# Moving a one-matmul fold of the sample rows' norm sums between two V column blocks of a gated layer

## Chip, cores and metric

The kernel runs on the 8 cores of one Trainium2 chip (two dies: cores 0 to 3 and 4 to 7). The metric is the device time of one execution in microseconds (us), that of the slowest core. A program on all cores has slow runs, in which one die is granted a lower TensorE clock; only fast runs are compared here.

## What is computed

Four layers of a decoder trunk. Layers 0 and 2 have a gated mixer: from `h` (1024 channels) come `u` and `v` (2048 each, after GELU), `v` is RMS-normed over its 2048 channels, mixed over the rows of a chunk of 128 rows, and gates `u`:

```python
z = jax.nn.gelu(jnp.einsum('btd,de->bte', h, w_in))
u, v = jnp.split(z, 2, axis=-1)
v = rmsnorm(v, g_v)                       # mean of squares over 2048 channels
# [...] masked mixing matrices ws, chunks of 128 rows
s = jnp.einsum('hij,bcjhe->bcihe', ws, vp) + bias
y = jnp.einsum('bte,ed->btd', u * s, w_out)
```

Each core has 2048 prompt rows, in two groups of 1024 (8 chunks of 128), and 64 "sample" rows, which form a short chunk of their own. The sample rows go with group 0, so their chunk occurs twice in the program: in layers 0 and 2 of group 0.

## The kernel before

The program is recorded as a list of operations. A list scheduler with modelled costs then gives every engine its order, and a wait is emitted for every dependency. The program treats PSUM, the memory that matmuls write, as eight banks of 512 fp32 columns. In the gated mixer four banks (4 to 7) hold the spatial sums of a chunk. V matmuls use the other four as two pairs: a "half" is 1024 columns of V (two column blocks of 512, eight matmuls each), and it takes one pair.

For a chunk of 128 rows: two halves of V, each followed by GELU and a square with its row sum on ScalarE; then the norm; then the spatial matmuls; then the gating product on VectorE. The sample rows' chunk is second in the list. It has only 64 rows, so both halves of its channels are stacked in the 128 partitions. The row sums of the two stacked halves then have to be added across partitions; a matmul with a 0/1 matrix does that. This is *the fold*: one matmul with two columns (the sum split in a high and a low bf16 part).

```python
# lines 1003 to 1023: a chunk of 128 rows
            for ci, (col0, nt, t) in enumerate(chunks):
                vb = vnb[ci % 2]
                vs = vstat[ci % 2]
                if nt == 128:
                    hv = []
                    for half in range(2):
                        bks = palloc(2, range(4), chain='v')
                        vx = vh[vx_turn % 3]
                        vx_turn += 1
                        hv.append(vx)

                        def mmv(e):
                            for q in range(2):
                                w = vu[2 * half + q]
                                for kc in range(KC):
                                    i = e.matmul(pap(bks, q * 512, (q + 1) * 512), lhsT=hB.t[:, kc, col0:col0 + nt], rhs=w.t[:, kc, :],
                                                 start=(kc == 0), stop=(kc == KC - 1))
                            return i
                        rec(PE, mmv, reads=vu[2 * half].all + vu[2 * half + 1].all + [hB.r[(kc, t)] for kc in range(KC)],
                            pt=[(bks, True)], cost=mmc(2 * KC, 512))
                        gelu_square(vx, bks, vs, half)
# [...] norm on POOL, two scalings on DVE
# lines 1031 to 1050: the sample rows' chunk
                else:
                    bks = palloc(2, range(4), chain='v')
                    vx = vh[vx_turn % 3]
# [...] mmvs: 32 matmuls, both channel halves stacked
                    rec(PE, mmvs, reads=sum((w.all for w in vu), []) + [hB.r[(kc, t)] for kc in range(KC)], pt=[(bks, True)], cost=mmc(2 * KC, 512) + 0.1)
                    gelu_square(vx, bks, vs, 0)
                    rec(DVE, lambda e: e.tensor_copy(out=hilo.t[:, 0:1], in_=vs.t[:, 0:1]), reads=vs.all, writes=hilo.all, cost=0.2)
                    rec(DVE, lambda e: e.tensor_tensor(out=hilo.t[:, 1:2], in0=vs.t[:, 0:1], in1=hilo.t[:, 0:1], op=ALU.subtract), reads=vs.all + hilo.all, writes=hilo.all, cost=0.2)
                    pf = palloc()
                    rec(PE, lambda e: e.matmul(pap(pf, 0, 2), lhsT=maskT.t[:, 1, :], rhs=hilo.t[:, :], start=True, stop=True), reads=hilo.all + maskT.all, pt=[(pf, True)], cost=0.07)
                    rec(DVE, lambda e: e.tensor_scalar(out=vs.t[:, 1:2], in0=pap(pf, 0, 1), scalar1=EPS, scalar2=None, op0=ALU.add), pt=[(pf, False)], reads=vs.all, writes=vs.all, cost=0.2)
                    rec(DVE, lambda e: e.tensor_tensor(out=vs.t[:, 2:3], in0=pap(pf, 1, 2), in1=vs.t[:, 1:2], op=ALU.add), pt=[(pf, False)], reads=vs.all, writes=vs.all, cost=0.2)
# [...] power on POOL, four scalings on DVE, a store
# then for every chunk: bias seed (ACT), spatial matmuls, gating product
                rec(PE, mms, reads=vb.all + (wsT if nt == 128 else msm).all, pt=[(sb, True)], cost=mmc(16, nt))
                rec(DVE, lambda e: e.tensor_tensor(out=ua, in0=pap(sb, 0, 16 * nt).rearrange("p (a b) -> p a b", b=nt), in1=ua, op=ALU.mult),
                    pt=[(sb, False)], reads=ur, writes=ur, cost=dvec(16 * nt))
```

`palloc()` asks for any free bank. The fold comes when banks 4 to 7 are taken by the spatial sums, so it takes one of the four V banks. (The program's own scheduler can be run without the chip and gives the banks in gated layer 0: the sample's V in 0 and 1, the first half after it in 2 and 3, the fold in 0, the second half in 2 and 3 again.)

Of the kernel before, what the change touches and what calls it, by code (L numbers as in the profile page):

```python
# [22 lines left out]
NSM = 64  # L23
KC = 8
# [334 lines left out]
def build_program():  # L359
# [41 lines left out]
    with es:  # L401
# [47 lines left out]
        hB = alloc("hB", [128, KC, NTMAX], BF16, pieces=[((k, t), k * NTMAX + sum(KW[:t]), k * NTMAX + sum(KW[:t + 1])) for k in range(KC) for t in range(3)])  # L449
# [55 lines left out]
        vstat = [alloc(f"vstat{i}", [128, 8], F32) for i in range(2)]  # L505
# [21 lines left out]
        rec = R.rec  # L527
# [3 lines left out]
        def palloc(n=1, allowed=range(8), chain=None):  # L531
            p = PTile(reg, n, [tuple(range(a, a + n)) for a in range(0, 8, n) if all(b in allowed for b in range(a, a + n))])
            if chain is not None:
                p.pred = chains.get(chain)
                chains[chain] = p
            return p

        def pap(p, lo=0, hi=512):
            return psum[:, p.b * 512 + lo:p.b * 512 + hi]
# [16 lines left out]
        def mmc(n, N):  # L556
            return n * (N / 2400.0 + 0.0025)
# [4 lines left out]
        def dvec(N, stt=False):  # L562
            return (0.215 if stt else 0.157) + N * 0.00104
# [312 lines left out]
        def mixer_a(g, l, after_tile):  # L876
# [123 lines left out]
                rec(ACT, lambda e: e.activation(out=junk.t[:, :], in_=vx.t[:, :], func=AF.Square, scale=float(DV) ** -0.5, accum_out=vs.t[:, col:col + 1]),  # L1000
                    reads=vx.all, writes=junk.all + vs.all, cost=actc(1024, False) + 0.2)

            for ci, (col0, nt, t) in enumerate(chunks):
                vb = vnb[ci % 2]
                vs = vstat[ci % 2]
                if nt == 128:
                    hv = []
                    for half in range(2):
                        bks = palloc(2, range(4), chain='v')
                        vx = vh[vx_turn % 3]  # L1010
                        vx_turn += 1
                        hv.append(vx)

                        def mmv(e):
                            for q in range(2):
                                w = vu[2 * half + q]
                                for kc in range(KC):
                                    i = e.matmul(pap(bks, q * 512, (q + 1) * 512), lhsT=hB.t[:, kc, col0:col0 + nt], rhs=w.t[:, kc, :],  # L1018
                                                 start=(kc == 0), stop=(kc == KC - 1))
                            return i  # L1020
                        rec(PE, mmv, reads=vu[2 * half].all + vu[2 * half + 1].all + [hB.r[(kc, t)] for kc in range(KC)],
                            pt=[(bks, True)], cost=mmc(2 * KC, 512))
                        gelu_square(vx, bks, vs, half)
                    rec(POOL, lambda e: e.tensor_scalar(out=vs.t[:, 2:3], in0=vs.t[:, 0:1], scalar1=vs.t[:, 1:2], scalar2=EPS, op0=ALU.add, op1=ALU.add), reads=vs.all, writes=vs.all, cost=0.3)
                    rsqrt_pool(vs.t[:, 2:3], vs.t[:, 3:4], vs.all, 1)
                    for half in range(2):
                        vx = hv[half]
                        hs = slice(half * 1024, (half + 1) * 1024)
                        rec(DVE, lambda e: e.scalar_tensor_tensor(out=vb.t[:, hs], in0=vx.t[:, :], scalar=vs.t[:, 3:4], in1=gvb.t[:, hs], op0=ALU.mult, op1=ALU.mult),  # L1029
                            reads=vx.all + vs.all + gvb.all, writes=[vb.r[half]], cost=dvec(1024, True))  # L1030
                else:
                    bks = palloc(2, range(4), chain='v')
                    vx = vh[vx_turn % 3]
                    vx_turn += 1

                    def mmvs(e):
                        for q in range(2):
                            for kc in range(KC):
                                for h in range(2):
                                    i = e.matmul(pap(bks, q * 512, (q + 1) * 512)[64 * h:64 * h + 64, :], lhsT=hB.t[:, kc, col0:col0 + nt], rhs=vu[2 * h + q].t[:, kc, :],  # L1040
                                                 start=(kc == 0), stop=(kc == KC - 1))
                        return i
                    rec(PE, mmvs, reads=sum((w.all for w in vu), []) + [hB.r[(kc, t)] for kc in range(KC)], pt=[(bks, True)], cost=mmc(2 * KC, 512) + 0.1)
                    gelu_square(vx, bks, vs, 0)
                    rec(DVE, lambda e: e.tensor_copy(out=hilo.t[:, 0:1], in_=vs.t[:, 0:1]), reads=vs.all, writes=hilo.all, cost=0.2)
                    rec(DVE, lambda e: e.tensor_tensor(out=hilo.t[:, 1:2], in0=vs.t[:, 0:1], in1=hilo.t[:, 0:1], op=ALU.subtract), reads=vs.all + hilo.all, writes=hilo.all, cost=0.2)
                    pf = palloc()
# [3 lines that stand above are left out]
                    rsqrt_pool(vs.t[:, 2:3], vs.t[:, 3:4], vs.all, 1)  # L1051
                    for dst_b in (vb, gout):
                        for h in range(2):
                            pr_ = slice(64 * h, 64 * h + 64)
                            rec(DVE, lambda e: e.scalar_tensor_tensor(out=dst_b.t[pr_, 0:1024], in0=vx.t[pr_, :], scalar=vs.t[pr_, 3:4], in1=gvb.t[pr_, 1024 * h:1024 * h + 1024],
                                                                      op0=ALU.mult, op1=ALU.mult),
                                reads=vx.all + vs.all + gvb.all, writes=dst_b.all[:1], cost=dvec(1024, True))
                    dma(SP, gmlp_v[j], gout.t[:], reads=gout.all, dsem=go_sem, nbytes=524288)
                ur = ubv[t].all
                uo = col0 - TILES[g][t][0]  # L1060
                ua = ubv[t].t[:, :, uo:uo + nt]
                for q in range(1 if nt == 128 else 2):
                    def seed(e):
                        if nt == 128:
                            return e.activation(out=pap(sb, 0, 2048).rearrange("p (h q t) -> p h q t", q=2, t=128),  # L1065
                                                in_=bsp.t[:, :, :].unsqueeze(2).to_broadcast([128, 8, 2, 128]), func=AF.Copy)
                        return e.activation(out=pap(sb, 0, 1024).rearrange("p (h q s t) -> p h q s t", q=2, s=NSEQ, t=4)[:, :, q],
                                            in_=bsp.t[:, :, 0:4].unsqueeze(2).to_broadcast([128, 8, NSEQ, 4]), func=AF.Copy)
                    rec(ACT, seed, pt=[(sb, True)], reads=bsp.all, cost=actc(2048 if nt == 128 else 512, False))

                def mms(e):
                    if nt == NSM:
                        for e8 in range(EC // 2):
                            for h in range(2):
                                pr_, ec = slice(64 * h, 64 * h + 64), 8 * h + e8
                                i = e.matmul(pap(sb, ec * nt, (ec + 1) * nt), lhsT=vb.t[pr_, e8 * 128:(e8 + 1) * 128], rhs=msm.t[pr_, e8 // 2, :], start=False, stop=True, skip_group_check=True)
                        return i
                    for ec in range(EC):
                        i = e.matmul(pap(sb, ec * nt, (ec + 1) * nt), lhsT=vb.t[:, ec * 128:(ec + 1) * 128], rhs=wsT.t[:, ec // 2, :], start=False, stop=True, skip_group_check=True)  # L1079
                    return i  # L1080
                rec(PE, mms, reads=vb.all + (wsT if nt == 128 else msm).all, pt=[(sb, True)], cost=mmc(16, nt))
                rec(DVE, lambda e: e.tensor_tensor(out=ua, in0=pap(sb, 0, 16 * nt).rearrange("p (a b) -> p a b", b=nt), in1=ua, op=ALU.mult),  # L1082
                    pt=[(sb, False)], reads=ur, writes=ur, cost=dvec(16 * nt))

            def mm_list(t, dc):
                w = unit(("Wo", g, l, dc // 2))
# [538 lines left out]
```

## Time and profile before

| | us |
|---|---|
| three timed runs | 3014.59, 2691.05, 2691.87 |
| the profiled execution | 2681.95 |
| span on its eight cores | 2677.5 to 2680.4, clock 0.999 to 1.000 |

From the page of the kernel before: the span, TensorE's busy time with its share, and the chain of work that ended last by engine. In these views PE is TensorE, PEld its weight loads, DVE VectorE, ACT ScalarE and POOL GpSimd; x8 means eight instructions in one line. The profiler models the ends of matmuls, so their starts are compared here and not their durations.

```profile
span 2680.4 us, 42477 instructions; the slowest of 8 cores (2677.5 to 2680.4 us)
...
PE 2668.4 (100%) x15797; PEld 1296.5 (48%) x15797; DVE 1382.1 (52%) x1740; ACT 1164.0 (43%) x1875; POOL 473.6 (18%) x968
...
PE 99%; DMA 1%; ACT 0%; issue 0%; POOL 0%; DVE 0%; DVEq 0%; ACTq 0%; POOLq 0%
```

The dies of the same execution:

```profile
die 0 (median of its cores): 2679.1 us, clock 1.000
die 1 (median of its cores): 2679.4 us, clock 1.000
```

TensorE is the bound, at full clock. What can be saved is time in which its stream has a hole. The stretch around the first sample chunk, from the timeline of core 5 (start in us, duration, engine, line, operation, output<-inputs; in brackets the idle time before it and what ended it):

```profile
91.19 1.89 PE L1018 MATMUL psum<-w_134,hB 128*128 128x512 bf16 x8
...
92.92 1.06 PE L1079 MATMUL psum<-wsT,vn_55 128*128 128x128 bf16 x16
93.18 1.02 ACT L998 ACTIVATE vh_114<-psum 128x1024 f32<-128x1024 f32 x1 [1.29 <-PE psum L1018]
...
93.81 0.17 PE L1048 MATMUL psum<-hilo,maskT 128*128 128x2 bf16 x1
94.08 2.29 DVE L1082 TENSOR_TENSOR UB_49<-psum,UB_49 128x2048 bf16<-128x2048 f32 x1 [1.61 <-PE psum L1048]
...
94.35 1.89 PE L1018 MATMUL psum<-w_135,hB 128*128 128x512 bf16 x8 [0.37 <-ACT vh_114 L998]
...
96.29 0.15 DVE L1049 TENSOR_SCALAR vstat_106<-psum 128x1 f32<-128x1 f32 x1
...
97.80 1.89 PE L1018 MATMUL psum<-w_133,hB 128*128 128x512 bf16 x8
```

Lines 1018 are the V matmuls: w_133 and w_134 are the two column blocks of the first half, w_135 and w_136 of the second. Line 1079 is the spatial matmuls of the chunk before, 1048 the fold, 998 the GELU, 1082 the gating product, 1049 the fold's first reader. A block is 1.73 us. The second half should start 0.89 us after the spatial matmuls (92.92); it starts after 1.43, having waited 0.37 us for the GELU of the first half. The waits of TensorE over the whole program (sum, number, longest) have this wait twice, under the last name:

```profile
engine line waited for: us in total, times, longest us
...
PE psum L1018 <- ACT vh_114 L998: 0.7, 2, 0.4
```

### The profile page before, as it was taken

To read this page: it belongs to the slowest core of one execution; us is meant where nothing else is said; L and a number is where in the kernel's file an instruction comes from. 1 tells how busy PE (TensorE), PEld (TensorE's weight loads), DVE (VectorE), ACT (ScalarE), POOL (GpSimd) and SP (SyncE) were. 2 spreads that over 40 slices of the span, in tenths; PEclk is the share of its full clock that TensorE was granted. 3 is DMA by queue.
4 is the path that set the end of the run, shared out by engine and by line. 5 is a ranking of instruction groups with operands and counts; after the bars stand their busy time and mean duration, and the time that the engine had idled before them with its cause. 6 is when DMAs were issued, how large, how long until landed. Compare 5 with 4: busy or idle time off the path is not lost.

```text
span 2680.4 us, 42477 instructions; the slowest of 8 cores (2677.5 to 2680.4 us)
## 1 busy us (share of the span) xinstructions
PE 2668.4 (100%) x15797; PEld 1296.5 (48%) x15797; DVE 1382.1 (52%) x1740; ACT 1164.0 (43%) x1875; POOL 473.6 (18%) x968
## 2 busy tenths in 40 slices
PE   9999999999999999999999999999999999999999
PEld 4554445544445444554444444444444444444445
DVE  4456534753335654375455565447541456526654
ACT  5634435642354443464336533345323634336432
POOL 1101223321010123333110000131100101013100
PEclk9999999999999999999999999999999999999999
DMA  9663335363444344427566335342544363334531
GB/s 194 126 113 63 68 64 99 73 103 73 80 87 82 64 77 84 87 49 120 107 129 142 63 67 93 62 79 53 97 89 81 62 119 66 62 54 81 96 55 64
DMA packets 41340, 229.47 MB, mean 86 GB/s; under 512 B 5584, under 2 KB 8016, under 8 KB 22416
## 3 DMA queue, kind: packets, MB, share of 16 engines
q0 software_dynamic: 33936, 197.39, 42.8%
q1 hardware_dynamic: 7056, 29.15, 3.2%
q8 instruction: 129, 2.11, 0.3%
q14 instruction: 75, 0.61, 0.1%
q10 hardware_dynamic: 144, 0.20, 0.0%
HBM read 408.29 MB, written 13.32 MB: 157 GB/s over the span
## 4 chain that ended last, share of the span: by engine, by line
PE 99%; DMA 1%; ACT 0%; issue 0%; POOL 0%; DVE 0%; DVEq 0%; ACTq 0%; POOLq 0%
PE psum L1276 45%; PE psum L821 31%; PE psum L1018 8%; PE psum L948 8%; PE psum L1318 2%; PE psum L1115 1%; PE psum L829 1%; PE psum L1079 1%; DMA xT_43<-x_in 1%; PE psum L957 1%; PE psum L1191 0%; PE psum L923 0%; PE psum L1040 0%; PE psum L1152 0%; PE psum L721 0%; PE psum L701 0%
## 5 line engine op out<-in xcount | busy, mean ns | idle before, releaser
L1298 DVE SCALAR_TENSOR_TENSOR cb_118<-psum,pvf,cb_118 128x510 f32<-128x510 f32 (+3 forms) x272 | 245.4, 903 | 137.7 <-POOL cb_118 L1296 61.3
L1298 DVE SCALAR_TENSOR_TENSOR cb_119<-psum,pvf,cb_119 128x511 f32<-128x511 f32 (+3 forms) x272 | 244.8, 904 | 101.0 <-POOL cb_119 L1296 43.9
L1288 ACT ACTIVATE cb_119<-psum,pvf 128x512 f32<-128x512 f32 (+1 forms) x136 | 122.5, 901 | 168.1 <-PE psum L1276 165.8
L1288 ACT ACTIVATE cb_118<-psum,pvf 128x512 f32<-128x512 f32 (+1 forms) x136 | 122.4, 900 | 140.0 <-PE psum L1276 129.2
L1301 ACT ACTIVATE cb_119<-cb_119 128x512 f32<-128x512 f32 (+1 forms) x136 | 102.2, 752 | 183.1 <-DVE cb_119 L1298 183.0
L832 DVE TENSOR_TENSOR xT_43<-psum,xT_43 128x512 f32<-128x512 f32 x96 | 66.3, 691 | 221.4 <-PE psum L821 221.4
L1302 DVE TENSOR_TENSOR mP<-cb_119,psum 128x512 bf16<-128x512 f32 (+1 forms) x136 | 114.7, 843 | 124.6 <-ACT cb_119 L1301 93.0
L1302 DVE TENSOR_TENSOR mP<-cb_118,psum 128x512 bf16<-128x512 f32 (+1 forms) x136 | 114.4, 842 | 104.6 <-ACT cb_118 L1301 71.4
L1301 ACT ACTIVATE cb_118<-cb_118 128x512 f32<-128x512 f32 (+1 forms) x136 | 102.1, 752 | 138.7 <-DVE cb_118 L1298 138.4
L832 DVE TENSOR_TENSOR xT_44<-psum,xT_44 128x512 f32<-128x512 f32 (+2 forms) x104 | 66.8, 648 | 161.4 <-PE psum L821 152.8
L1029 DVE SCALAR_TENSOR_TENSOR vn_55<-vh_114,vstat_105,gvb 128x1024 bf16<-128x1024 f32 x14 | 18.0, 1283 | 142.4 <-POOL vstat_105 L866 142.4
L675 ACT ACTIVATE sq_74<-xT_44 128x512 f32<-128x512 f32 (+1 forms) x61 | 37.7, 619 | 110.1 <-DVE xT_44 L832 105.0
L675 ACT ACTIVATE sq_75<-xT_43 128x512 f32<-128x512 f32 x58 | 36.2, 624 | 98.1 <-DVE xT_43 L832 90.7
L745 DVE SCALAR_TENSOR_TENSOR hB<-xT_43,pvd,rstd_81 128x512 bf16<-128x512 f32 x88 | 62.1, 775 | 28.6 <-ACT rstd_81 L725 24.4
L1065 ACT ACTIVATE psum<-bsp 128x2048 f32<-128x2048 bf16 x32 | 60.2, 1880 | 29.2 <-DVE UB_49 L1082 14.7
L675 ACT ACTIVATE sq_74<-xT_43 128x512 f32<-128x512 f32 x54 | 33.7, 625 | 89.2 <-DVE xT_43 L832 80.2
L745 DVE SCALAR_TENSOR_TENSOR hB<-xT_44,pvd,rstd_82 128x512 bf16<-128x512 f32 x96 | 64.9, 745 | 13.9 <-ACT rstd_82 L725 10.2
L835 ACT ACTIVATE hB<-xT_43,pvd 128x512 bf16<-128x512 f32 x32 | 23.1, 721 | 109.1 <-DVE xT_43 L832 109.1
L675 ACT ACTIVATE sq_75<-xT_44 128x512 f32<-128x512 f32 (+1 forms) x54 | 33.4, 618 | 78.5 <-DVE xT_44 L832 74.2
L1082 DVE TENSOR_TENSOR UB_49<-psum,UB_49 128x2048 bf16<-128x2048 f32 x16 | 36.7, 2292 | 38.0 <-PE psum L1079 34.8
L1082 DVE TENSOR_TENSOR UB_50<-psum,UB_50 128x2048 bf16<-128x2048 f32 x16 | 36.6, 2290 | 28.0 <-PE psum L1079 28.0
L938 ACT ACTIVATE UB_49<-psum 128x512 bf16<-128x512 f32 x56 | 32.2, 595 | 39.6 <-PE psum L948 38.3
(1129 smaller groups left out, 5605.5 us busy)
## 6 DMA issues: line engine op xcount, KB each, us to landing
ASb<-st_conv SPq DMA_DIRECT2D x4, 1056.0 KB, 10.9
gvb<-g_v SPq DMA_DIRECT2D x4, 1024.0 KB, 13.0
hPS<-st_pool SPq DMA_DIRECT2D x2, 1248.0 KB, 6.5
xT_44<-x_in POOLq DMA_DIRECT2D x4, 512.0 KB, 10.5
xs_113<-x_in SPq DMA_DIRECT2D x2, 1024.0 KB, 6.1
y_out<-yT_52 SPq DMA_DIRECT2D x2, 1024.0 KB, 7.6
xT_44<-x_in SPq DMA_DIRECT2D x2, 1024.0 KB, 8.0
y_out<-yT_53 SPq DMA_DIRECT2D x2, 1024.0 KB, 11.8
```

The costliest lines, as they stand in the source:

```text
L675: rec(ACT, lambda e: e.activation(out=d, in_=x, func=AF.Square), reads=xr(t, kc, lo, hi), writes=wr, cost=actc(n, False))
L745: last = rec(DVE, lambda e: e.scalar_tensor_tensor(out=hB.t[:, kc, c0:c0 + n], in0=xb.t[:, kc, :], scalar=pvd.t[:, kc, gidx:gidx + 1], in1 ...
L821: ins = e.matmul(pap(bk, 0, hi - lo), lhsT=mms[i][0], rhs=mms[i][1][:, lo:hi], start=(i == 0), stop=(i == nm - 1))
L832: rec(DVE, lambda e: e.tensor_tensor(out=xv[t].t[:, dc, lo:hi], in0=pap(bk, 0, hi - lo), in1=xv[t].t[:, dc, lo:hi], op=ALU.add), pt=[(bk, ...
L948: i = e.matmul(pap(bks[e4], 0, n), lhsT=ub.t[:, kc, e4 * 128:(e4 + 1) * 128], rhs=hB.t[:, kc, c0:c0 + n], start=(kc == 0), stop=(kc == KC ...
L1018: i = e.matmul(pap(bks, q * 512, (q + 1) * 512), lhsT=hB.t[:, kc, col0:col0 + nt], rhs=w.t[:, kc, :], start=(kc == 0), stop=(kc == KC - 1))
L1082: rec(DVE, lambda e: e.tensor_tensor(out=ua, in0=pap(sb, 0, 16 * nt).rearrange("p (a b) -> p a b", b=nt), in1=ua, op=ALU.mult), pt=[(sb, F ...
L1276: i = e.matmul(pap(bk, i_ * TN, i_ * TN + TN), lhsT=w.t[:, kc, fs], rhs=hB.t[:, kc, c0:c0 + TN], start=(kc == 0), stop=(kc == KC - 1))
L1288: rec(ACT, lambda e: e.activation(out=cb.t[:, o:o + N], in_=pap(gb, 0, N), func=AF.Identity, bias=sc(12 + l, fc), scale=sc(3 * l + 2, fc)) ...
L1298: rec(DVE, lambda e: e.scalar_tensor_tensor(out=cb.t[:, o + sh:o + N], in0=pap(gb, 0, N - sh), scalar=sc(3 * l + 2 - sh, fc), in1=cb.t[:, ...
L1301: rec(ACT, lambda e: e.activation(out=cb.t[:, o:o + N], in_=cb.t[:, o:o + N], func=AF.Silu), reads=cw, writes=cw, cost=actc(N, False), tab ...
L1302: rec(DVE, lambda e: e.tensor_tensor(out=mP.t[:, ts[0]:ts[-1] + 1, fc, :], in0=cb.t[:, o:o + N].rearrange("p (t c) -> p t c", c=TN), in1=p ...
```

## The change

The intent: let the second half's first column block go ahead of the fold, in the sample's pair of banks. By the time of the fold the pair of the first half has been emptied by its GELU, so the fold finds a bank there and makes nobody wait. The work after the V matmuls of a chunk becomes a function `finish`, called at once for the 128-row chunks and later for the sample rows:

```diff
-            for ci, (col0, nt, t) in enumerate(chunks):
-                vb = vnb[ci % 2]
-                vs = vstat[ci % 2]
+            def finish(col0, nt, t, vb, vs, hv):
 # [...] norm, fold, scalings, seed, spatial matmuls, gating product: unchanged
+            late = None
+            for ci, (col0, nt, t) in enumerate(chunks):
 # [...]
+                        for qs in ((0,), (1,)) if half and late is not None else ((0, 1),):
+                            def mmv(e):
+                                for q in qs:
 # [...] eight matmuls of column block q
+                            rec(PE, mmv, reads=sum((vu[2 * half + q].all for q in qs), []) + [hB.r[(kc, t)] for kc in range(KC)], pt=[(bks, True)], cost=mmc(len(qs) * KC, 512))
+                            if len(qs) == 1 and late is not None:
+                                finish(*late)
+                                late = None
+                        gelu_square(vx, bks, vs, half)
 # [...] the sample rows' V matmuls, GELU and square: unchanged
+                if nt == NSM:
+                    late = (col0, nt, t, vb, vs, hv)
+                    continue
+                finish(col0, nt, t, vb, vs, hv)
```

More of the change, by code (lines that the diff above doesn't have):

```diff
@@ L1001, in gelu_square @@
                     reads=vx.all, writes=junk.all + vs.all, cost=actc(1024, False) + 0.2)
-            for ci, (col0, nt, t) in enumerate(chunks):
-                vb = vnb[ci % 2]
-                vs = vstat[ci % 2]
+            def finish(col0, nt, t, vb, vs, hv):
                 if nt == 128:
-                    hv = []
-                    for half in range(2):
-                        bks = palloc(2, range(4), chain='v')
-                        vx = vh[vx_turn % 3]
-                        vx_turn += 1
-                        hv.append(vx)
-                        def mmv(e):
-                            for q in range(2):
-                                w = vu[2 * half + q]
-                                for kc in range(KC):
-                                    i = e.matmul(pap(bks, q * 512, (q + 1) * 512), lhsT=hB.t[:, kc, col0:col0 + nt], rhs=w.t[:, kc, :],
-                                                 start=(kc == 0), stop=(kc == KC - 1))
-                            return i
-                        rec(PE, mmv, reads=vu[2 * half].all + vu[2 * half + 1].all + [hB.r[(kc, t)] for kc in range(KC)],
-                            pt=[(bks, True)], cost=mmc(2 * KC, 512))
-                        gelu_square(vx, bks, vs, half)
                     rec(POOL, lambda e: e.tensor_scalar(out=vs.t[:, 2:3], in0=vs.t[:, 0:1], scalar1=vs.t[:, 1:2], scalar2=EPS, op0=ALU.add, op1=ALU.add), reads=vs.all, writes=vs.all, cost=0.3)
@@ L1031, in mixer_a @@
                 else:
-                    bks = palloc(2, range(4), chain='v')
-                    vx = vh[vx_turn % 3]
-                    vx_turn += 1
-                    def mmvs(e):
-                        for q in range(2):
-                            for kc in range(KC):
-                                for h in range(2):
-                                    i = e.matmul(pap(bks, q * 512, (q + 1) * 512)[64 * h:64 * h + 64, :], lhsT=hB.t[:, kc, col0:col0 + nt], rhs=vu[2 * h + q].t[:, kc, :],
-                                                 start=(kc == 0), stop=(kc == KC - 1))
-                        return i
-                    rec(PE, mmvs, reads=sum((w.all for w in vu), []) + [hB.r[(kc, t)] for kc in range(KC)], pt=[(bks, True)], cost=mmc(2 * KC, 512) + 0.1)
-                    gelu_square(vx, bks, vs, 0)
+                    vx = hv[0]
                     rec(DVE, lambda e: e.tensor_copy(out=hilo.t[:, 0:1], in_=vs.t[:, 0:1]), reads=vs.all, writes=hilo.all, cost=0.2)
@@ L1083, in mixer_a, with mmvs @@
                     pt=[(sb, False)], reads=ur, writes=ur, cost=dvec(16 * nt))
+            late = None
+            for ci, (col0, nt, t) in enumerate(chunks):
+                vb = vnb[ci % 2]
+                vs = vstat[ci % 2]
+                if nt == 128:
+                    hv = []
+                    for half in range(2):
+                        bks = palloc(2, range(4), chain='v')
+                        vx = vh[vx_turn % 3]
+                        vx_turn += 1
+                        hv.append(vx)
+                        for qs in ((0,), (1,)) if half and late is not None else ((0, 1),):
+                            def mmv(e):
+                                for q in qs:
+                                    w = vu[2 * half + q]
+                                    for kc in range(KC):
+                                        i = e.matmul(pap(bks, q * 512, (q + 1) * 512), lhsT=hB.t[:, kc, col0:col0 + nt], rhs=w.t[:, kc, :],
+                                                     start=(kc == 0), stop=(kc == KC - 1))
+                                return i
+                            rec(PE, mmv, reads=sum((vu[2 * half + q].all for q in qs), []) + [hB.r[(kc, t)] for kc in range(KC)], pt=[(bks, True)], cost=mmc(len(qs) * KC, 512))
[3 more added lines that the diff above has]
+                        gelu_square(vx, bks, vs, half)
+                else:
+                    bks = palloc(2, range(4), chain='v')
+                    vx = vh[vx_turn % 3]
+                    vx_turn += 1
+                    def mmvs(e):
+                        for q in range(2):
+                            for kc in range(KC):
+                                for h in range(2):
+                                    i = e.matmul(pap(bks, q * 512, (q + 1) * 512)[64 * h:64 * h + 64, :], lhsT=hB.t[:, kc, col0:col0 + nt], rhs=vu[2 * h + q].t[:, kc, :],
+                                                 start=(kc == 0), stop=(kc == KC - 1))
+                        return i
+                    rec(PE, mmvs, reads=sum((w.all for w in vu), []) + [hB.r[(kc, t)] for kc in range(KC)], pt=[(bks, True)], cost=mmc(2 * KC, 512) + 0.1)
+                    gelu_square(vx, bks, vs, 0)
+                    hv = [vx]
+                if nt == NSM:
+                    late = (col0, nt, t, vb, vs, hv)
+                    continue
+                finish(col0, nt, t, vb, vs, hv)
```

## The prediction

> **What bounds the kernel.** TensorE. The page gives it 2668.4 us busy of a span of 2680.4; the chain that ended last is 99% TensorE. In the timeline a block of eight 512-column V matmuls starts 1.73 us after the one before, 216 ns a matmul; the Trainium skill ("TensorE: Matmul & The Clock Gate", "Wait, 56ns, not 53.3ns?") gives 215.7 for a warm array, so the stream is at its floor. The table of cores shows clock 1.000. Only holes in TensorE's stream are to be had.
>
> **The hole aimed at.** The sample rows' chunk occurs twice (group 0, two gated layers, near 86 and 771 us). Timeline of the first: chunk 1's first V half has its second column block at 91.19, chunk 0's spatial matmuls start at 92.92, the fold (one 128x2 matmul) at 93.81, chunk 1's second V half only at 94.35. TensorE's waits put 0.37 us of that down to ScalarE's GELU of the first half (93.18, 1.02 us long). Why: V halves alternate between two pairs of PSUM banks; the spatial sums hold the other four banks. The fold takes a bank of the sample's pair and holds it until VectorE, busy with a 2.29 us gating product, reads it at 96.29. So the second half must take the pair that the first half has just filled, and waits for its GELU. Without a fold between (112.06 to 112.95) spatial matmuls to next V block take 0.89 us; here 1.43. The fold costs 0.54 us each time.
>
> **What the change does.** No arithmetic is added or removed. The second half's first column block follows the spatial matmuls at once (93.82), in the sample's pair, whose GELU ended at 90.64. The fold follows at about 95.55 in a bank of the first half's pair, freed at 94.2; then the second column block. The fold still costs, by an estimate from 55 ns per spatial matmul (16 in 0.89 us) and its 98 ns weight load, 0.06 to 0.12 us. Net 0.42 to 0.48 a layer, 0.9 us in all.
>
> **Does it reach the end?** VectorE is in its gating product until 96.37 either way, so the fold's readers, the sample's four scalings (to 102.5) and the next GELU, which waited 2.33 us for them, stay put. That GELU ends at 103.7; its banks are needed at 105.1 before, 104.7 after: 1 us of slack remains. The fold's bank is free at 96.7 and wanted at 97.4. TensorE's later waits list nothing that could give the gain back. So I expect all of it, 0.03%: hardly above the scatter (fast runs 2691.05, 2691.87).
>
> **Predicted: 2690.6 us**, 8 in 10 between 2687 and 2694. Faster by over 2%: 0.01; within: 0.97; slower: 0.02 (two slow runs of three).
>
> **What would show it right.** The 0.37 us wait of the V matmuls for the GELU is gone, twice; the fold stands between the column blocks, adding at most 0.12 us to their 1.73; TensorE runs 0.4 to 0.5 us earlier after the first layer, 0.8 to 1.0 after the second; the fold's readers are still held by the gating product.
>
> **What would make it wrong.** The order comes from a list scheduler with modelled costs: half a microsecond moved can reorder later work, by some microseconds either way. The fold's bank might come free late, so that chunk 2's first half waits instead. Or the sample's scalings hold chunk 2's GELU long enough to stall TensorE.

## The result, and the profile after

| | all timed runs, us | median |
|---|---|---|
| before, 6 runs (the three above and three more) | 3014.59, 2691.05, 2691.87, 2691.42, 2772.12, 2820.85 | 2731.99 |
| after, 6 runs | 2691.52, 2917.78, 2687.14, 2917.2, 2690.34, 2691.3 | 2691.41 |

The two medians can't be compared: three of the six runs before fell in the slow state and two of those after. The fast runs alone have a ratio of 0.9995, with a 95% interval of 0.9975 to 1.0015: the same time. (A ratio is the mean time of one kernel's fast runs over that of the other's of the same rounds, so not quite the ratio of quoted medians.)

The page of the changed kernel and its dies:

```profile
span 2689.7 us, 42475 instructions; the slowest of 8 cores (2677.8 to 2689.7 us)
...
PE 2680.4 (100%) x15797; PEld 1300.0 (48%) x15797; DVE 1382.2 (51%) x1740; ACT 1163.7 (43%) x1875; POOL 475.2 (18%) x968
...
PE 99%; DMA 1%; issue 0%; ACT 0%; POOL 0%; DVE 0%; DVEq 0%; ACTq 0%; POOLq 0%
```

```profile
die 0 (median of its cores): 2678.0 us, clock 0.999
die 1 (median of its cores): 2686.6 us, clock 0.996
```

The span of the slowest core is 9 us longer than before, and TensorE's busy time 12 us. That is not the change: die 1 ran at a clock of 0.996 in this execution, 0.3% below the other die, and 0.3% of 2680 is 8 us. Undisturbed die 0 has 2678.0 against 2679.1 before. The trace shows how: the clock of core 7 is full but for the ends of the program and 14 stretches of 3.4 to 5.8 us, 68 us in all, where it is 0.8125 (shown as 0.81) and 512-column matmuls start 263 ns apart, not 216. By an estimate these stretches cost 68 x (1 - 0.8125) = 13 us; core 7 is 11.7 us longer than the median of die 0. The first one (the stretch in us, its length, PE's busy time and matmuls, the clock, then DMA):

```profile
200.00:212.20 12.20, 12.20 (x73) 1.00 0.90 140
212.20:217.00 4.80, 4.80 (x20) 0.81 0.14 31
```

So the rest is read from core 0, at clock 0.999.

The timeline of core 0 after the change (line numbers moved: 1071 V matmuls, 1048 spatial matmuls, 1017 fold, 1018 and 1019 its readers, 1051 gating product):

```profile
89.44 1.89 PE L1071 MATMUL psum<-w_134,hB 128*128 128x512 bf16 x8
...
91.17 1.06 PE L1048 MATMUL psum<-wsT,vn_55 128*128 128x128 bf16 x16
91.43 1.02 ACT L998 ACTIVATE vh_114<-psum 128x1024 f32<-128x1024 f32 x1 [1.29 <-PE psum L1071]
...
92.06 1.89 PE L1071 MATMUL psum<-w_135,hB 128*128 128x512 bf16 x8
92.33 2.29 DVE L1051 TENSOR_TENSOR UB_49<-psum,UB_49 128x2048 bf16<-128x2048 f32 x1 [1.60 <-PE psum L1048]
...
93.58 0.10 PEld L1017 LDWEIGHTS psum<-hilo,maskT 128*128 128x128 bf16 x1
93.79 0.17 PE L1017 MATMUL psum<-hilo,maskT 128*128 128x2 bf16 x1
...
93.82 1.89 PE L1071 MATMUL psum<-w_136,hB 128*128 128x512 bf16 x8
94.54 0.15 DVE L1018 TENSOR_SCALAR vstat_106<-psum 128x1 f32<-128x1 f32 x1
...
94.79 0.16 DVE L1019 TENSOR_TENSOR vstat_106<-psum,vstat_106 128x1 f32<-128x1 f32 x1
...
95.54 1.67 PE L1071 MATMUL psum<-w_133,hB 128*128 128x512 bf16 x6
```

The second half's first block (w_135) now follows the spatial matmuls after 0.89 us. The fold is at 93.79, 1.73 us later, and the second block (w_136) starts 0.03 us after it. From the spatial matmuls to the next chunk's V it is 4.37 us (91.17 to 95.54) where it was 4.88 (92.92 to 97.80). TensorE's waits on core 0 no longer have the GELU among the V matmuls; what is left at their line is two short ones without a named releaser, of a kind that core 0 had before too (two, 0.3 us in all, beside its GELU wait):

```profile
engine line waited for: us in total, times, longest us
...
PE psum L1071 <- issue: 0.3, 2, 0.2
```

Between the two kernels, TensorE's order differs in two places only, the two folds; no later operation was reordered.

A finer measure than the time of an execution is the distance between two fixed points of one core's trace. I take *the interval*: from the start of the first sample-row V matmul of layer 0 to that of layer 2. One fold and the 128-row chunk after it lie in it. Before: 685.11 to 685.12 us on all eight cores. After: 684.61 us on all four cores of die 0 (on slowed die 1 686.25 to 686.50). Starts are printed to 0.01 us, and where the clock is full it repeats to that (E4 and E5 have exceptions, explained there), so the gain per layer is 0.50 us.

### The profile page after: what moved, and what is told of

Read it like the earlier page. It is cut to its first block, busy times and chain, and to the rows that moved or that the text cites. A ratio compares the mean times of both kernels' runs of the same rounds, so it can differ in the third digit from the quotient of the medians.

```text
span 2689.7 us, 42475 instructions; the slowest of 8 cores (2677.8 to 2689.7 us)
## 1 busy us (share of the span) xinstructions
PE 2680.4 (100%) x15797; PEld 1300.0 (48%) x15797; DVE 1382.2 (51%) x1740; ACT 1163.7 (43%) x1875; POOL 475.2 (18%) x968
## 4 chain that ended last, share of the span: by engine, by line
PE 99%; DMA 1%; issue 0%; ACT 0%; POOL 0%; DVE 0%; DVEq 0%; ACTq 0%; POOLq 0%
PE psum L1290 45%; PE psum L821 31%; PE psum L1071 8%; PE psum L948 8%; PE psum L1332 2%; PE psum L1048 1%; PE psum L1129 1%; PE psum L829 1%; PE psum L957 0%; DMA xT_43<-x_in 0%; PE psum L1205 0%; PE psum L923 0%; DMA xT_44<-x_in 0%; PE psum L1088 0%; PE psum L1166 0%; PE psum L721 0%
## 5 line engine op out<-in xcount | busy, mean ns | idle before, releaser
L835 ACT ACTIVATE hB<-xT_43,pvd 128x512 bf16<-128x512 f32 x32 | 23.1, 722 | 109.2 <-DVE xT_43 L832 109.2
L835 ACT ACTIVATE hB<-xT_44,pvd 128x512 bf16<-128x512 f32 x32 | 23.1, 721 | 63.2 <-DVE xT_44 L832 48.8
```

## Experiments

Nine kernels ran on the chip. E1 is the changed kernel again; the others keep every engine's order apart from the edit named (checked by comparing instruction orders). All intervals are of cores at a clock of 0.999 or more, from one trace a run. Slow executions are left out: 3082.94 us in E1, 2979.27 in E2, 2815.79 and 2996.83 in E5, 3046.29 in E7. Theory: *the bank*. The fold takes a bank of the sample's pair, so the second half has to take the pair just filled, and waits for its GELU. Rivals: the fold's own matmul is dear beside the short spatial matmuls; the split of the half matters and not the fold's place; any later place is as good; the gain or loss is a matter of clocks or of the scheduler.

| run | interval, us | against before |
|---|---|---|
| before | 685.11 to 685.12 | |
| after (die 0), E1 (all cores) | 684.61; 684.59 to 684.61 | -0.51 |
| E2 split only, fold ahead | 685.10 to 685.11 | 0 |
| E3 no fold | 684.57 to 684.58 | -0.54 |
| E4 nine folds between the blocks | 684.79 to 684.87, seven of eight within 0.01 of 684.80 | -0.31 |
| E5 nine folds ahead | 685.10 to 685.21 | 0 to +0.10 |
| E6 fold after the whole half | 685.44 to 685.45 | +0.33 |
| E7 GELU late, fold ahead | 686.27 to 686.28 | +1.16 |
| E8 GELU late, fold between (die 0) | 684.67 to 684.69 | -0.43 |
| E9 bank taken, no fold matmul | 685.10 to 685.11 | 0 |

### E1: the changed kernel again, five rounds

No edit.

> The changed kernel once more, five rounds beside the kernel before. Measure used in all runs: TensorE's time from the first sample-row V matmul of gated layer 0 to that of gated layer 2, on cores with a granted clock of 0.999 or more: 685.11 us before, 684.61 after (traces at hand). My theory: the gain is 0.50 us a layer, about 1.0 us in all, so fast runs stand at a ratio of 0.9996, and anything larger between single runs is the clock of a die. Rival (scheduler or clock effect of the change): fast runs differ by several us in one direction, and the cores with a lower clock appear only with the changed kernel.

On chip 11 (the record doesn't name the chip of the runs above): six runs of this kernel, 2681.01 to 2682.53 us and one slow at 3082.94; eleven of the kernel before, of which three slow. The ratio of fast runs is 0.9982, interval 0.9937 to 1.0027, wide because one run before, 2712.60, counts as fast though two of its cores were at a clock of 0.986. Taking only executions in which every core had 0.999 or more: seven before with a mean of 2682.54 us, five after with 2681.66, so 0.88 us less. The single runs scatter by 1.0 and 0.7 us (standard deviation), so the times alone would not carry this; the mean over all their cores, 2679.47 and 2678.50, says 0.97. The lower clock came with the kernel before too (2712.60), so it is not a matter of the change. The expectation held.

The gain also reaches the end. From the first sample-row V matmul to the end of the program, the mean of eight cores is 2594.60 us in the trace before, 2594.57 in E2 (which has the old order), and 2593.70 in E1: 0.90 less. The part up to layer 2 gives 0.51 of it, the rest 0.38. The rest holds the second fold, which gains as much at its own place (778.03 to 782.91 is 4.88 us before; 778.04 to 782.41 is 4.37 after, on cores 5 and 7, which have full clock there); the last stretch of the program has waits that differ from core to core by about a microsecond, so these totals are good to perhaps 0.1 us.

### E2: the split alone

```diff
+for qs in ((0,), (1,)) if half and g == 0 and ci == 2 else ((0, 1),):
     def mmv(e):
-        for q in range(2):
+        for q in qs:
# the fold stays recorded ahead of the half
```

> The kernel before with only the split: the second V half after the sample rows is recorded as two column blocks, the fold stays ahead of both. Bank theory (the fold's bank makes the second half wait for the first half's GELU): nothing changes, 685.11 us, wait of 0.37 us for the GELU still there. Rival (the gain comes from the split, an earlier release between the blocks): 684.6 us.

685.10 to 685.11 us, and the 0.37 us wait for the GELU is still there, twice (core 2, V matmuls now in line 1019):

```profile
PE psum L1019 <- ACT vh L998: 0.7, 2, 0.4
```

Splitting does nothing by itself.

### E9: the bank without the matmul

```diff
-rec(PE, lambda e: e.matmul(pap(pf, 0, 2), lhsT=maskT.t[:, 1, :], rhs=hilo.t[:, :], start=True, stop=True), ...)
+rec(DVE, lambda e: e.memset(pap(pf, 0, 2), 0.5), reads=hilo.all, pt=[(pf, True)], cost=0.07)
# readers kept behind the gating product as before; modelled cost of the half + 0.07
```

Its output is wrong, which doesn't matter for the time.

> The fold's matmul taken away but its bank kept at the old place: VectorE writes the two columns instead (wrong sample rows on purpose). Bank theory: TensorE's second half still takes the first half's pair and still waits for its GELU, now about 0.54 us, 685.08 to 685.11 us. Rival (the fold's matmul itself is dear beside the short spatial matmuls, its weight load exposed, the queue drained): the hole is gone, 684.58 us, as without a fold.

The interval is that of the kernel before, with no fold matmul on TensorE at all. The timeline of core 2 (1080 spatial matmuls, 999 GELU, 1019 V matmuls):

```profile
94.15 1.06 PE L1080 MATMUL psum<-wsT,vn 128*128 128x128 bf16 x16
...
94.41 1.02 ACT L999 ACTIVATE vh<-psum 128x1024 f32<-128x1024 f32 x1 [1.29 <-PE psum L1019]
...
95.58 0.59 PE L1019 MATMUL psum<-w,hB 128*128 128x512 bf16 x2 [0.37 <-ACT vh L999]
```

The second half starts 1.43 us after the spatial matmuls, exactly as before, and waits 0.37 us for the GELU. (I had expected 0.54 us of named wait; the view counts from the modelled end of the matmul before, which is no earlier without the fold.) So the cost was the bank. A fold that costs TensorE nothing would have cost the kernel the same.

### E3: neither bank nor matmul

```diff
-pf = palloc()
-rec(PE, ... the fold ...)
-rec(DVE, ... in0=pap(pf, 0, 1) ...); rec(DVE, ... in0=pap(pf, 1, 2) ...)
+rec(DVE, ... in0=hilo.t[:, 0:1] ...); rec(DVE, ... in0=hilo.t[:, 1:2] ...)   # sums of one stacked half, wrong on purpose
# readers and modelled cost as in E9
```

> The fold's matmul and its bank taken away, wrong sample rows on purpose, all other orders kept. Both theories: no GELU wait, and what is left against the changed kernel is the cost of the fold between the blocks: 684.58 us if it is the 0.03 us that the changed kernel's timeline shows, 684.50 to 684.55 if it is the 0.06 to 0.12 of my prediction.

684.57 to 684.58 us. So the fold cost 0.54 us before and costs 0.03 now; of all that could be had, the change takes 94% (0.51 of 0.54).

### E4: nine folds between the blocks

```diff
-rec(PE, ... one matmul ...)
+for _ in range(9): i = e.matmul(pap(pf, 0, 2), lhsT=maskT.t[:, 1, :], rhs=hilo.t[:, :], start=True, stop=True)
```

> The changed kernel with the fold done nine times between the column blocks. Here no wait hides them: the interval rises by eight times what one fold really costs TensorE. At 0.03 us: 684.85; at the 0.06 to 0.12 of my prediction: 685.1 to 685.6.

684.80 us: eight more folds cost 0.19 us, 24 ns each (0.20 us, 25 ns each, against E1, which ran on the same chip). The timeline of core 1:

```profile
95.03 0.37 PE L1019 MATMUL psum<-hilo,maskT 128*128 128x2 bf16 x9
95.26 0.59 PE L1075 MATMUL psum<-w,hB 128*128 128x512 bf16 x2
```

The first fold starts 0.23 us before the next block, for nine. In the traces a single fold has a duration of 167 ns; that is not what it takes from the stream.

### E5: nine folds ahead of the second half

The same nine in the kernel before.

> The kernel before with the fold's matmul done nine times in a row (same result). Bank theory: TensorE has to wait for the GELU anyway, so the eight further folds run in the hole; at 0.03 to 0.06 us each they take 0.24 to 0.48 us of 0.37, and the interval rises by 0 to 0.15 us, to 685.11 to 685.26. Rival (the fold itself costs the 0.54 us, or 0.17 of it, at that place): it rises by 8 times 0.17 to 0.54, to 686.5 or more.

Five cores of eight lie at 685.10 to 685.15, the others up to 685.21. What some cores have above 685.11 does not arise at the fold: compared start by start with core 0, they lose it (0.04 to 0.10 us) at a small matmul of layer 1, 341 us after the interval's start; so does the odd core of E4 (0.07 us). The nine folds (93.85 below) run while TensorE has to wait for the GELU anyway; the wait shrinks from 0.37 to 0.17 us and the second half starts 1.42 us after the spatial matmuls, as before. The timeline of core 2:

```profile
92.96 1.06 PE L1083 MATMUL psum<-wsT,vn 128*128 128x128 bf16 x16
93.85 0.37 PE L1050 MATMUL psum<-hilo,maskT 128*128 128x2 bf16 x9
94.38 0.59 PE L1018 MATMUL psum<-w,hB 128*128 128x512 bf16 x2 [0.17 <-ACT vh L998]
```

### E6: the fold one block later still

```diff
-for qs in ((0,), (1,)) if half and late is not None else ((0, 1),):
+for qs in ((0, 1),):
-    if len(qs) == 1 and late is not None:
+    if half and late is not None:
         finish(*late)
```

> The fold after the whole second half, ahead of the next chunk's first half. Bank theory: the fold then takes a bank of the first half's pair just when the next chunk wants that pair, and TensorE waits for the fold's two readers on VectorE, 0.4 to 0.7 us: 685.0 to 685.3 us, wait named VectorE. Rival (any later place is as good, what counts is that the fold is not ahead of the second half): 684.6 us.

The direction was right, the size was not: 685.44 us, beyond the range that I gave, and 0.33 worse than before. The timeline of core 5:

```profile
92.92 3.62 PE L1071 MATMUL psum<-w,hB 128*128 128x512 bf16 x16
93.19 2.29 DVE L1051 TENSOR_TENSOR UB<-psum,UB 128x2048 bf16<-128x2048 f32 x1 [1.62 <-PE psum L1048]
...
96.38 0.17 PE L1017 MATMUL psum<-hilo,maskT 128*128 128x2 bf16 x1
96.69 0.16 DVE L1018 TENSOR_SCALAR vstat<-psum 128x1 f32<-128x1 f32 x1 [1.20 <-PE psum L1017]
...
96.95 0.16 DVE L1019 TENSOR_TENSOR vstat<-psum,vstat 128x1 f32<-128x1 f32 x1
...
97.25 2.10 PE L1071 MATMUL psum<-w,hB 128*128 128x512 bf16 x9 [0.71 <-DVE vstat L1019]
```

After the second half the fold takes a bank of the first half's pair, and the next chunk's first half wants that pair at once. It starts 0.87 us after the fold. I had counted the two readers on VectorE, but not the 0.31 us from the fold's start to its first reader (96.38 to 96.69), nor the 0.14 us from the end of the second reader to TensorE (96.95 + 0.16 to 97.25). Here nobody else holds VectorE (the gating product ended at 95.48), so the hole is all hand-over. "Later" alone is thus no recipe.

### E7 and E8: the GELU late

In both kernels one more ScalarE read of the first half's sums is put ahead of their GELU:

```diff
+if g == 0 and ci == 2 and half == 0:
+    rec(ACT, lambda e: e.activation(out=junk.t[:, :], in_=pap(bks, 0, 1024), func=AF.Copy), pt=[(bks, False)], writes=junk.all, cost=0.0)
 gelu_square(vx, bks, vs, half)
```

> The kernel before with one more ScalarE read of the first half's sums (1024 columns, about 1.05 us) ahead of their GELU. Bank theory: the second half's start moves with the GELU, the wait grows from 0.37 to about 1.4 us, 686.1 to 686.2 us. Rival: 685.11, ScalarE has slack.

With the old order the interval grows by 1.16 us and the wait of the V matmuls to 1.54, slightly more than I expected, as the added read holds the GELU for 1.17 us and not 1.05. In the timeline of core 1 the GELU starts 1.17 us after the added read, and the second half's start moves with it:

```profile
94.40 1.02 ACT L1024 ACTIVATE junk<-psum 128x1024 bf16<-128x1024 f32 x1 [1.29 <-PE psum L1018]
...
95.03 0.17 PE L1050 MATMUL psum<-hilo,maskT 128*128 128x2 bf16 x1
...
95.57 1.02 ACT L998 ACTIVATE vh<-psum 128x1024 f32<-128x1024 f32 x1
...
96.74 0.59 PE L1018 MATMUL psum<-w,hB 128*128 128x512 bf16 x2 [1.54 <-ACT vh L998]
```

> The changed kernel with the same further ScalarE read ahead of the first half's GELU. Bank theory: the GELU then ends at about 0.3 us before the fold wants its bank, so nothing waits and the interval stays 684.61 us (at most 0.1 more): the changed order has over 1 us of slack there. Rival (the change only shifted a wait that any ScalarE delay brings back): 685.6 us.

With the new order the same delay costs 0.07 us (684.67 to 684.69 on die 0; die 1 was slowed in this execution and is left out, and so is its single time of 2718.88 us; the kernel before took 2711.01 in the same round, on chip 0, with cores 4 and 5 at 0.988 and 0.987). The timeline of core 0:

```profile
90.58 1.02 ACT L1079 ACTIVATE junk<-psum 128x1024 bf16<-128x1024 f32 x1 [1.29 <-PE psum L1071]
...
91.21 1.89 PE L1071 MATMUL psum<-w,hB 128*128 128x512 bf16 x8
...
91.75 1.02 ACT L998 ACTIVATE vh<-psum 128x1024 f32<-128x1024 f32 x1
...
93.03 0.16 PE L1017 MATMUL psum<-hilo,maskT 128*128 128x2 bf16 x1
...
93.05 3.18 PE L1071 MATMUL psum<-w,hB 128*128 128x512 bf16 x13
```

The GELU ends at 92.77; the fold would have been due at 92.94 (1.73 after the block before) and starts at 93.03. I had reckoned with 0.3 us to spare; it was 0.17 before the fold was due, and from the GELU's end to the start of a matmul that waited for it the kernel before needs 0.15 us as well (94.20 to 94.35); the fold's weights are now loaded only at 92.99, where the changed kernel has them 0.21 us ahead of the fold. So the slack of the new order is, by this estimate, about 1.1 us of ScalarE delay.

No experiment points to a version that would beat the changed kernel at this place: without any fold, only 0.03 us a layer would be left to gain.

## Why the prediction was right and where it failed

**What bounds it, and the hole: right.** The bank is the cause (E9), not the matmul (E5, E9) and not the split (E2). The wait for the GELU is the mechanism (E7). The prediction read this from two lines of the timeline and the bank layout. The program keeps a second writer out of a bank until its readers are done, as the Trainium skill ("PSUM — Partial Sum Buffer", section "PSUM bank collisions raise a hardware error") advises: to guard PSUM by bank and quadrant of 32 partitions, or more simply by bank. No run here tries what happens without; and as a V block fills all 512 columns of its bank, here it would also overwrite the fold's sums.

**What the change does: right in kind, one term mis-sized.** "The fold still costs, by an estimate from 55 ns per spatial matmul (16 in 0.89 us) and its 98 ns weight load, 0.06 to 0.12 us." It costs 0.03 us (timeline, E3), 24 to 25 ns for a further one (E4). The weight load adds nothing, since it lies under the stream of the block before it: in the timeline after the change, it starts 0.21 us ahead of the fold, under the running block (93.58, the line PEld 1017). I had the right figure at hand and used another: the Trainium skill ("TensorE: Matmul & The Clock Gate", section "Wait, 56ns, not 53.3ns?") says that start to start "never drops below ≈25 ns however small N is", and a matmul of two columns is that case; E4 agrees. So the net is 0.50 to 0.51 us a layer and not 0.42 to 0.48. Twice that is 1.0, and 0.9 to 1.0 is what E1 shows over the program, so the sum of 0.9 was close.

**Does it reach the end: right.** Nothing was reordered, and no wait on another compute engine was added to TensorE's list (two cores of E1 wait 0.7 and 0.8 us for V weights, a load; on the core looked at this is ahead of the first sample chunk). The fold's first reader is still held by the gating product (94.54, while the product runs from 92.33 for 2.29 us), and the bank is free before the next first half (95.54). E6 shows what happens where that guard fails.

**The base of the time: this failed.** The step is "hardly above the scatter (fast runs 2691.05, 2691.87)": I took these timed runs as the level of the kernel, to subtract 0.9 from, and gave a range of 2687 to 2694. The same material had a profiled execution at 2681.95 us with full clock on all cores, 10 us below, and I didn't ask why. The runs of the changed kernel answer it: its fast runs of 2687.14 to 2691.52 all have cores of die 1 at 0.995 to 0.998, and in the traced one (2691.52) these means come from stretches at 0.8125 that are worth about 12 us on the slowest core; with full clock everywhere (E1, chip 11) it takes 2681.0 to 2682.5, outside my range. That the median after, 2691.41, came within 0.8 us of 2690.6 is luck: die 1 was slowed in those runs. So the step took for the level of the kernel a time 9 us above the one at full clock (2682.54 on average in E1). That the kernel before was at 2691 for the same reason is likely but not shown, as the clocks of those runs were not recorded; that it can happen to that kernel is shown by its 2711.01 (E8) and 2712.60 us (E1). I also gave 0.02 to an answer spoilt by slow runs, though one run of three had already been slow; in the end three of six before and two of six after were. Set against the six-run median before, 2731.99, my 2690.6 reads as a forecast of -1.5%, when the change is worth -0.03 to -0.04%. The forecast should have been a difference, 0.9 us between runs of equal clocks, and the time a separate statement about the state of the chip.

## What to carry to other kernels

When a tiny operation needs a buffer that big ones alternate between, its price is the wait that it makes the next big one take, not its own length: look for the place where a buffer of the rotation is free and will not be wanted until the tiny one's reader is through; here one step earlier cost 0.54 us and one step later 0.87, and at the right place it cost 0.03. An effect of half a microsecond can be shown on a program of 2.7 ms if two fixed points of the trace are compared on cores at full clock, where the distance repeats to 0.01 us. Before predicting a time, check that the profiled execution and the timed ones are at the same clock.

## What the Trainium skill lacked or had wrong

- "TensorE: Matmul & The Clock Gate", the note on the peak-current limiter: it says that dense matmuls on three cores take the whole die to 13/16 of the clock (0.8125) for as long as the load lasts, and to budget for that. Here eight cores run them almost without a hole for 2.68 ms, and 21 of the 38 executions with recorded clocks have means of 0.999 or 1.000 on all cores. The level agrees, the rest does not: in the two kept traces with a slowed die (the changed kernel's and E8's) the clock is 0.8125 only in stretches of 3.4 to 8.1 us, with full clock between, and each pair of cores has its own: cores 4 and 5 have 5 stretches and 6 and 7 have 14 in the one, 42 and 8 in the other. No trace of a slow execution (means of 0.83 to 0.96 on a die) was kept, and no run tells what sets a stretch off.
- The same page, "Back-to-back issue gap": it gives a sustained spacing of about 81 ns at 128 columns and 131 ns at 512 for pairs of weight load and matmul. Here it is 56 ns (0.89 us for 16 spatial matmuls) and 216 ns (1.73 us for 8), each matmul with its own weight load; these agree with the figures that the page gives for back-to-back matmuls (55.6 and 215.7 ns).
- "Perfetto Trace Analysis", section "Tensor Engine Instruction (MATMUL, LD_WEIGHTS)": it says that a matmul's end is estimated from its size, but not that the duration shown for a small one is several times what it takes from the stream. The fold is shown with 167 ns, which is what the TensorE page's section "Single matmul latency" gives for one alone ((398 + 2) / 2.4), and takes 24 to 25 ns of the stream (E4).
- None of the pages read (these and that on PSUM) says what a hand-over between engines costs in PSUM use: here 0.15 us from the end of a GELU to a matmul in its bank, and 0.31 us from the start of a two-column matmul to VectorE's read of it.
